# 128 instead of 96 tokens by gathered rows in an expert layer, and a ranking moved ahead of the transposes

## The chip, the core and the metric

The kernel runs on one core of a Trainium2 chip, as one launch. The metric is the device time of the launch in microseconds. The core has a matrix engine (PE, with its weight loads listed apart as PEld), a vector engine (DVE), a scalar engine (ACT), a general engine (POOL) and a queue that only issues transfers (SP). Each engine runs its instructions in program order. Sixteen DMA engines move the data; POOL's transfers stand in queue q0 (software), those of SP in q1 and those of ACT in q10 (hardware).

## What is computed

The reference is two transformer blocks on 512 tokens of width 1024. The change lies in the feed-forward layer of the first block, a layer of 16,384 experts. Each expert `e` has a row `u[e]` and a row `v[e]` of 1024 numbers:

```python
q = (xb @ wq).reshape(C, 8, 2, 64)
s = einsum('chpd,hpnd->chpn', q, keys)            # two lists of 128 scores per head
sv, si = top_k(s, 16)
cand = sv[:, :, 0, :, None] + sv[:, :, 1, None, :]
top_s, sel = top_k(cand.reshape(C, 8, 256), 16)   # 16 experts per head: 128 per token
g = softmax(top_s)
act = gelu(einsum('chkd,cd->chk', u_tab[eidx], xb))
out = einsum('chk,chkd->cd', g * act, v_tab[eidx])
```

## The kernel before

Products are made in two halves of each operand (high and low part), three matmuls for one. All weights come through one stream: SP loads a piece (`wr`), ACT casts its high part (`wh`, L119), DVE or POOL subtracts for the low part (`wl`, L121).

The expert layer treats tokens in two ways. **Dense tokens** (`TD`) are multiplied with all 16,384 experts, in 128 chunks of 128 experts, and the 128 wanted experts of a token are picked by a matrix `G` that is zero elsewhere. **Gathered tokens** (`GROUPS`, the last tokens) fetch only their own rows: an indirect DMA by POOL brings 128 rows of 4 KB (`row`, L935), and DVE does a dot product with it (`u` rows, L949) or adds it, weighted, to a sum (`v` rows, L958). A group of `n` tokens with `P` copies fills 128 partitions and needs 128/P such steps for `u` and as many for `v`: (64, 2) needs 64 + 64, and (32, 4) needs 32 + 32, so 192 steps before. The steps are a generator; `gstep()` does one of them at chosen places. One step keeps `GB - 1` = 2 loads ahead.

The layer has these stages, in program order:

- **The ahead stage.** For 84 of the chunks `u_chunk` multiplies the dense tokens with `u` (24 matmuls, L269, L270, L272), ACT applies gelu (L910), and the result is put away in DRAM (`ad`). Between chunks the generator `routing()` is pumped: it yields an estimate of DVE time after each part, and each chunk buys `BUD` of it; a `gstep` (at chunks whose number modulo 6 is in `GR`) costs 1.9. What is left when the chunks end is run off in a loop without chunks (`while live`). Routing goes through four tiles of 128 tokens, 3, 0, 1, 2. For each it ranks (`top16`, two heads at a time), decodes the winners to expert numbers (`id01`, with ACT's help at L1041 and L1045), lets PE transpose them (L1078), and builds for each 16 dense tokens four one-hot arrays on DVE (L1095 to L1101), from which PE makes a piece of `G` (`build_g`, 32 matmuls, L1113 and L1114); ACT evacuates it (L1115) and writes it to DRAM (`gd`). Tile 3 comes first because the gathered tokens lie in it: `pick` (L921) hands their expert numbers to the gathers.
- **The run stage.** Of the 44 fresh chunks, five `u_chunk`s open it. Then 16 runs of 8 chunks each follow, with the other 39 fresh chunks between their passes. A run has two passes over `v` (`v_pass`, 96 matmuls each at L260 to L262, one for each half of the width): a run in the middle of the stage is a pass, two fresh chunks, a pass, one fresh chunk. `load_g` loads the run's part of `G` (`gt`, on POOL's queue) a run ahead, `w_prod` (L1175) and `w_split` (L252, L253) make the weights of the experts, and DVE adds the products to the tokens (`hT`, L1206). A `gstep` follows each fresh chunk and those chunks of a pass that are in `GV`.
- Before the last pass, `while gat: gstep()` runs off the gather steps that are left, and the last of them ends in 8 or 16 matmuls on PE (L963) that fold the copies together.

Of the kernel before, what the change touches and what calls it, by code (L numbers as in the profile page):

```python
# [9 lines left out]
F32 = mybir.dt.float32  # L10
# [35 lines left out]
PRE = 2  # L46
BUD = 5.0
NA = 4
# [10 lines left out]
SUB = 16  # L59
GROUPS = ((64, 2), (32, 4))  # L60
TD = T - sum(n for n, _ in GROUPS)
NSB = TD // SUB
GR = (0, 3)
GB = 3
# [7 lines left out]
GP_ = 2  # L72
# [19 lines left out]
PA = tuple(range(6))  # L92
GV = (1, 2, 4, 6)

# [47 lines left out]
def _body(tc, nc, V, S, PE, GP, A, out, upto, tap, ctx):  # L142
# [106 lines left out]
    def split(hi, lo, src, g):  # L249

        if g is None:
            S.copy(hi, src)  # L252
            V.tensor_tensor(lo, src, r32(hi), op=OP.subtract)  # L253
        else:
            S.activation(hi, src, AF.Copy, scale=g)
            V.scalar_tensor_tensor(lo, src, g, r32(hi), op0=OP.mult, op1=OP.subtract)
# [88 lines left out]
    def xtile(p, h="xh", l="xl", n=8, c=T, bufs=None):  # L345
        return p.tile([128, n, c], F32R, name=h, bufs=bufs), p.tile([128, n, c], F32R, name=l, bufs=bufs)
# [429 lines left out]
    with ExitStack() as st:  # L776
        with st0 as st1:
            with ExitStack() as st2:
# [57 lines left out]
                if upto <= 1:  # L836
                    return dump()
                xnh, xnl = xtile(xp)
                gx = pool(st, "gx", side="right")
# [21 lines left out]
                def norm_x(k):  # L861
                    tn = xq.tile([128, T], F32, name="tn", bufs=2)
                    V.scalar_tensor_tensor(tn, H[k], col("g_ffn", k), rB[:, :T], op0=OP.mult, op1=OP.mult)
                    split(xnh[:, k], xnl[:, k], tn, None)
                    for a, (t0, n, P) in enumerate(groups):
                        V.tensor_copy(xg[:, a, k].rearrange("p (b t) -> p b t", b=P),
                                      tn[:, None, t0:t0 + n].to_broadcast([128, P, n]))
# [122 lines left out]

            def route(i):

                sv = wk.tile([128, 8, 2, 16], F32, name="sv", bufs=1)
                si = wk.tile([128, 8, 2, 16], U32, name="si", bufs=1)
                ts = wk.tile([128, 8, 16], F32, name="ts", bufs=1)
                tp = wk.tile([128, 8, 16], U32, name="tp", bufs=1)
                for h in range(0, 8, 2):
                    ch = []
# [20 lines left out]
                    top16(ch)  # L1019
                    yield 3.0  # L1020

                tpf = tp.rearrange("p h k -> p (h k)")
# [42 lines left out]
                V.tensor_tensor(ge, ge, gs[:, 1, :, None].to_broadcast([128, 8, 16]), op=OP.mult)  # L1065
                yield BUD
                if i == 3:
# [51 lines left out]
            def routing():  # L1119
                late = []  # L1120
                for i in (3, 0, 1, 2):
                    tk = yield from route(i)
                    for s in range(min(8, NSB - 8 * i)):
                        a = yield from onehots(tk, s)
                        late.append((i, s) + a)
                        if len(late) > 1:
                            build_g(*late.pop(0))
                for a in late:
                    build_g(*a)
# [30 lines left out]
        def load_g(r):  # L1160
            if r < len(runs):
                gt[r] = pk.tile([128, NSB, RUN, SUB], F32, name="gt", bufs=2)
                for b in range(0, NSB, NSB // GP_):
                    sl = slice(b, b + NSB // GP_)
                    nc.gpsimd.dma_start(gt[r][:, sl].rearrange("p b i t -> p b (i t)"),
                                        gd[sl, :, RUN * r:RUN * (r + 1)].rearrange("b p i t -> p b (i t)"))
# [738 lines left out]
```

## Time and profile before

| | |
|---|---|
| median of 3 runs | 2871.4 us (2870.38 to 2872.52) |
| the profiled execution, its time | 2870.35 us |
| its span, first to last instruction | 2868.2 us |
| PE busy | 2758.8 us, 96% |
| DVE busy | 1905.4 us, 66% |
| ACT busy | 1193.5 us, 42% |
| POOL busy | 876.0 us, 31% |
| moved by DMA | 457.17 MB, mean 159 GB/s |

Time outside the span is 2.15 us in the profiled execution. A busy share is a mean over stages that have different limits, so each stage is read by itself.

### The profile page before, as it was taken

The page shows a single profiled execution, that of the slowest core. Times are in us where ns is not written, and L with a number is a line of the kernel's source. Part 1 is how long each engine was busy: PE and PEld are TensorE (multiplying, and loading weights), DVE is VectorE, ACT ScalarE, POOL GpSimd, SP SyncE. Part 2 cuts the span into 40 slices and gives each one's busy share as a digit, 9 for nine tenths or more (in the row PEclk, how much of TensorE's full clock was granted, in tenths as well). Part 3 has the DMA queues.
Part 4 walks back from the last instruction along what each step waited for, and adds up shares of the span by engine and source line. Part 5 has one row for each costly group of instructions (what it writes and reads, how often), then busy time and mean ns, then how long its engine had stood idle before and what let it go on. Part 6 is the DMA issues. An engine that isn't in the chain of part 4 may idle for free. (4 is left out here: it accounts for less than half of the span.)

```text
span 2868.2 us, 38216 instructions
## 1 busy us (share of the span) xinstructions
PE 2758.8 (96%) x14308; PEld 2429.1 (85%) x14308; DVE 1905.4 (66%) x3477; ACT 1193.5 (42%) x1962; POOL 876.0 (31%) x521
## 2 busy tenths in 40 slices
PE   8778998999999999999999999999999999999998
PEld 7646898999989999999999988888887866788887
DVE  5887599798957867777778765444436489544433
ACT  5564543646553333343333423332223378433322
POOL 3653155555534456564456000000003133000000
PEclk9889999999999999999999999999999999999999
DMA  3102255767678888888888333333234200233332
GB/s 126 52 8 66 70 175 179 262 193 259 211 278 305 285 295 281 306 283 280 294 296 301 99 101 96 96 97 100 91 101 141 81 23 1 74 99 100 96 94 83
DMA packets 156568, 457.17 MB, mean 159 GB/s; under 512 B 17056, under 2 KB 40864, under 8 KB 152800
## 3 DMA queue, kind: packets, MB, share of 16 engines
q1 hardware_dynamic: 103008, 273.33, 29.5%
q0 software_dynamic: 36704, 135.54, 14.2%
q10 hardware_dynamic: 16672, 45.88, 4.0%
q8 instruction: 112, 1.84, 0.3%
q14 instruction: 72, 0.59, 0.1%
HBM read 407.43 MB, written 47.25 MB: 159 GB/s over the span
## 5 line engine op out<-in xcount | busy, mean ns | idle before, releaser
L119 ACT CAST wh<-wr 128x1024 fp32r<-128x1024 f32 (+1 forms) x356 | 369.4, 1038 | 394.4 <-issue 206.3
L121 DVE TENSOR_TENSOR wl<-wr,wh 128x1024 fp32r<-128x1024 f32 (+1 forms) x231 | 287.5, 1245 | 368.1 <-ACT wh L119 363.4
L121 POOL TENSOR_TENSOR wl<-wr,wh 128x1024 fp32r<-128x1024 f32 x125 | 334.0, 2673 | 330.2 <-ACT wh L119 325.4
L262 PE MATMUL m<-xh,wl 128*128 128x512 f32 x1080 | 422.2, 391 | 3.4 <-POOL wl L121 2.7
L260 PE MATMUL m<-xh,wh 128*128 128x512 f32 x1080 | 424.4, 393 | 0.0
L261 PE MATMUL m<-xl,wh 128*128 128x512 f32 x1048 | 407.9, 389 | 0.0
L269 PE MATMUL m<-xh,wh 128*128 128x416 f32 x1024 | 365.0, 356 | 9.7 <-ACT stg L1115 5.8
L261 PE MATMUL d<-wtl,vh 128*128 128x416 f32 x1024 | 359.5, 351 | 2.6 <-DVE wtl L253 2.6
L260 PE MATMUL d<-wth,vh 128*128 128x416 f32 x1024 | 359.8, 351 | 1.8 <-DVE hT L1206 0.9
L270 PE MATMUL m<-xl,wh 128*128 128x416 f32 x1024 | 360.9, 352 | 0.0
L262 PE MATMUL d<-wth,vl 128*128 128x416 f32 x1024 | 359.1, 351 | 0.2
L121 DVE TENSOR_TENSOR vl<-vr,vh 128x512 fp32r<-128x512 f32 x256 | 174.7, 688 | 140.1 <-ACT vh L119 133.9
L262 PEld LDWEIGHTS m<-xh,wl 128*128 128x128 f32 x1080 | 203.2, 188 | 49.4 <-DVE wl L121 3.4
L260 PEld LDWEIGHTS m<-xh,wh 128*128 128x128 f32 x1080 | 203.2, 188 | 43.3 <-issue 1.2
L119 ACT CAST vh<-vr 128x512 fp32r<-128x512 f32 x256 | 153.9, 619 | 206.1 <-DMA vr<-in_vr 148.5
L261 PEld LDWEIGHTS m<-xl,wh 128*128 128x128 f32 x1048 | 196.8, 188 | 41.2 <-issue 1.0
L935 POOL DMA_INDIRECT row<-in_vr,gix x96 | 174.6, 1818 | 141.0 <-DVE xt L958 109.3
L272 PE MATMUL m<-xh,wl 128*128 128x416 f32 x1024 | 213.3, 350 | 0.0
L910 ACT ACTIVATE act<-m 128x416 f32<-128x416 f32 x128 | 66.4, 519 | 343.3 <-PE m L272 336.5
L269 PEld LDWEIGHTS m<-xh,wh 128*128 128x128 f32 x1024 | 194.9, 190 | 15.8 <-ACT stg L1115 10.2
L261 PEld LDWEIGHTS d<-wtl,vh 128*128 128x128 f32 x1024 | 192.3, 188 | 5.5 <-DVE wtl L253 3.8
L260 PEld LDWEIGHTS d<-wth,vh 128*128 128x128 f32 x1024 | 192.2, 188 | 5.1 <-ACT act L910 1.3
(428 smaller groups left out, 5378.5 us busy)
## 6 DMA issues: line engine op xcount, KB each, us to landing
wr<-in_u SPq DMA_DIRECT2D x128, 512.0 KB
vr<-in_vr SPq DMA_DIRECT2D x256, 256.0 KB
wr<-in_w_gu SPq DMA_DIRECT2D x88, 512.0 KB
gd<-stg ACTq DMA_DIRECT2D x26, 1024.0 KB
gt<-gd POOLq DMA_DIRECT2D x32, 832.0 KB
ad<-act ACTq DMA_DIRECT2D x84, 208.0 KB
act<-ad SPq DMA_DIRECT2D x84, 208.0 KB
wr<-in_w_down SPq DMA_DIRECT2D x32, 512.0 KB
```

The lines of the kernel that those rows point to most:

```text
L119: nc.scalar.copy(hi[:, :n], t[:, :n])
L121: eng.tensor_tensor(lo[:, :n], t[:, :n], hi[:, :n].bitcast(F32), op=OP.subtract)
L260: PE.matmul(ps, lhsT=wh, rhs=xh, start=first, stop=False)
L261: PE.matmul(ps, lhsT=wh, rhs=xl, start=False, stop=False)
L262: PE.matmul(ps, lhsT=wl, rhs=xh, start=False, stop=last)
L269: PE.matmul(ps, lhsT=wh, rhs=xhs[k], start=k == 0, stop=False)
L270: PE.matmul(ps, lhsT=wh, rhs=xls[k], start=False, stop=False)
L272: PE.matmul(ps, lhsT=w[1][:, wc + k * 128:wc + k * 128 + 128], rhs=xhs[k], start=False, stop=k == n - 1)
L910: S.activation(a, ps, AF.Gelu)
L935: GP.indirect_dma_start(out=g, out_offset=None, in_=A["vr" if v else "ur"], in_offset=bass.IndirectOffsetOnAxis(ap=gix[:, a, j:j + 1], axi ...
```

## The change

One group of 32 gathered tokens becomes one of 64, so that all of tile 3 is gathered, the dense tokens go from 416 to 384, and the gather steps from 192 to 256. The places of gather steps are set closer (`GR`, `GV`), the budget of a chunk is made smaller (`BUD`), and `route` is cut into three generators (`rank`, `decode`, `turn`), so that the first two heads of the next tile are ranked between a tile's decoding and its transposes. The wait that a whole `BUD` stood for at the end of decoding becomes 1.0.

```diff
-BUD = 5.0
+BUD = 4.7
...
-GROUPS = ((64, 2), (32, 4))
+GROUPS = ((64, 2), (64, 2))
...
-GR = (0, 3)
+GR = (0, 2, 3, 5)
...
-GV = (1, 2, 4, 6)
+GV = (1, 2, 4, 5, 7)
...
-                xnh, xnl = xtile(xp)
+                xnh, xnl = xtile(xp, c=TD)
...
-                    split(xnh[:, k], xnl[:, k], tn, None)
+                    split(xnh[:, k], xnl[:, k], tn[:, :TD], None)
...
-                yield BUD
+                yield 1.0
+                return id01
+
+            def turn(i, id01):
+
                 if i == 3:
...
             def routing():
                 late = []
-                for i in (3, 0, 1, 2):
-                    tk = yield from route(i)
+                tiles = (3, 0, 1, 2)
+                yield from rank(3, range(0, 8, 2))
+                for n, i in enumerate(tiles):
+                    id01 = yield from decode(i)
+                    nxt = tiles[n + 1] if n < 3 else None
+                    if nxt is not None:
+                        yield from rank(nxt, (0,))
+                    tk = yield from turn(i, id01)
                     for s in range(min(8, NSB - 8 * i)):
                         a = yield from onehots(tk, s)
                         late.append((i, s) + a)
                         if len(late) > 1:
                             build_g(*late.pop(0))
+                    if nxt is not None:
+                        yield from rank(nxt, range(2, 8, 2))
                 for a in late:
                     build_g(*a)
```

`load_g` rounds its two parts up, which changes nothing at 24 pieces of 16 tokens (26 before).

**DVE, between the decoding of tile 0 and its one-hots.** Rows of before, then of the change: `id` holds the decoded expert numbers, `tk` their transposed copy, and L981 to L989 rank.

```order
L1064 RECIPROCAL gs<-gs 128x8
L1065 TENSOR_TENSOR id_4085<-id_4085,gs 128x128
L1082 SCALAR_TENSOR_TENSOR tk<-m,tk 128x128
L1095 TENSOR_TENSOR o_4257<-iop,tk 128x2048
L1097 TENSOR_TENSOR o_4258<-iop,tk 128x2048
L1099 TENSOR_TENSOR oh<-o_4258,tk 128x2048
L1101 TENSOR_TENSOR ol<-o_4258,tk 128x2048
```

```order
L1073 TENSOR_TENSOR id_4049<-id_4049,gs 128x128
L949 SCALAR_TENSOR_TENSOR row,gdt<-row,xt 128x1024
L981 MAX sv<-z_2392 128x8 x2
L983 MATCH_REPLACE tmp<-sv,z_2392 128x128 x2
L985 MAX_INDEX si<-sv,z_2392 128x8 x2
L987 MAX sv<-tmp 128x8 x2
L989 MAX_INDEX si<-sv,tmp 128x8 x2
L949 SCALAR_TENSOR_TENSOR row,gdt<-row,xt 128x1024
```

The ranking of tile 1's first two heads and two gather steps now stand between the last row of `id` and the row that reads the transposes (`tk`, L1094 now), 22 rows later instead of one.

**PE, at the last tile's transposes.** Before, these rows stand behind the 74th of the 84 chunks of the ahead stage, and a chunk follows. In the change they stand behind the 84th, and the pieces of `G` follow each other from there on (nine of them, L1125 and L1126 now) up to the first fresh chunk.

```order
L272 MATMUL m<-xh,wl 128x416 x8
L1078 MATMUL m<-ident,id_6962 128x128 x3
L269 MATMUL m<-xh,wh 128x416
L270 MATMUL m<-xl,wh 128x416
L269 MATMUL m<-xh,wh 128x416
```

```order
L272 MATMUL m<-xh,wl 128x384 x8
L1090 MATMUL m<-ident,id_7293 128x128 x3
L1125 LDWEIGHTS o_6781
L1125 MATMUL m<-oh,o_6781 128x128
L1126 LDWEIGHTS o_6781
L1126 MATMUL m<-ol,o_6781 128x128
```

So all eight one-hot sets of the last tile are made with no chunk left to run beside them; before, it was three of the four arrays of the last set.

**DVE, between the last two passes.** Before and in the change, from the last `v` split of the pass ahead to the first rows of the last pass; `xt` is the sum that a gather step of `v` adds to.

```order
L121 TENSOR_TENSOR vl<-vr,vh 128x512
L1206 TENSOR_TENSOR hT<-d,hT 128x2x416 x2
L966 TENSOR_TENSOR hT<-m,hT 128x8x32
L121 TENSOR_TENSOR wl<-wr,wh 128x1024
L121 TENSOR_TENSOR vl<-vr,vh 128x512 x2
```

```order
L958 SCALAR_TENSOR_TENSOR xt<-row,gdt,xt 128x1024
L1227 TENSOR_TENSOR hT<-d,hT 128x2x384 x2
L958 SCALAR_TENSOR_TENSOR xt<-row,gdt,xt 128x1024 x12
L966 TENSOR_TENSOR hT<-m,hT 128x8x64
L121 TENSOR_TENSOR wl<-wr,wh 128x1024
L121 TENSOR_TENSOR vl<-vr,vh 128x512 x2
```

Twelve gather steps, none before, are now run off in a row there; on PE the fold matmuls that wait for the last of them stand ahead of the last pass, before as in the change.

## Rows read from the trace of the kernel before

**Rows 1.** The page: span, and busy time of each engine.

```profile
span 2868.2 us, 38216 instructions
PE 2758.8 (96%) x14308; PEld 2429.1 (85%) x14308; DVE 1905.4 (66%) x3477; ACT 1193.5 (42%) x1962; POOL 876.0 (31%) x521
```

**Rows 2.** Busy time in five stretches, with PE's granted clock, DMA share, GB/s.

```profile
core 0: us, PE busy (x) PEld busy (x) DVE busy (x) ACT busy (x) POOL busy (x), PEclk, DMA share, GB/s
355.00:815.00 460.00, 436.43 (x2758) 422.21 (x2757) 397.80 (x1076) 233.15 (x288) 251.39 (x110) 0.98 0.65 215
815.00:830.00 15.00, 11.09 (x107) 10.23 (x105) 7.42 (x7) 11.80 (x14) 0.00 (x0) 0.77 0.89 332
848.00:1598.00 750.00, 745.42 (x3959) 736.30 (x3959) 568.23 (x807) 272.49 (x463) 396.12 (x232) 1.00 0.84 288
1000.00:1020.00 20.00, 20.00 (x108) 19.85 (x107) 13.67 (x21) 5.47 (x10) 6.36 (x6) 1.00 1.01 348
1400.00:1500.00 100.00, 100.00 (x533) 99.25 (x532) 75.11 (x111) 34.67 (x61) 49.34 (x30) 1.00 0.89 299
```

**Rows 3.** What PE waited for from 360 to 860: total us, times, longest.

```profile
PE m L1078 <- DVE id L1060: 9.6, 3, 4.9
```

**Rows 4.** Timeline of ACT in the ahead stage: start, length, instruction, idle before.

```profile
356.68 0.52 ACT L910 ACTIVATE act<-m 128x416 f32<-128x416 f32 x1 [1.26 <-PE m L272]
361.20 0.52 ACT L910 ACTIVATE act<-m 128x416 f32<-128x416 f32 x1 [2.48 <-PE m L272]
...
616.28 0.52 ACT L910 ACTIVATE act<-m 128x416 f32<-128x416 f32 x1 [2.50 <-PE m L272]
...
628.81 0.52 ACT L910 ACTIVATE act<-m 128x416 f32<-128x416 f32 x1 [5.61 <-PE m L272]
...
635.66 0.52 ACT L910 ACTIVATE act<-m 128x416 f32<-128x416 f32 x1 [0.62 <-PE m L272]
...
814.89 0.52 ACT L910 ACTIVATE act<-m 128x416 f32<-128x416 f32 x1 [0.63 <-PE m L272]
...
829.70 1.05 ACT L119 CAST wh<-wr 128x1024 fp32r<-128x1024 f32 x1 [0.40 <-ACT stg L1115]
```

**Rows 5.** Timeline of PE: three rows of equal matmuls, each row's first and last.

```profile
60.96 0.28 PE L398 MATMUL d<-xh,wh 128*128 128x264 f32 x1
...
64.48 0.28 PE L400 MATMUL d<-xh,wl 128*128 128x264 f32 x1
...
1099.76 0.35 PE L262 MATMUL d<-wth,vl 128*128 128x416 f32 x1
...
1103.93 0.35 PE L260 MATMUL d<-wth,vh 128*128 128x416 f32 x1
...
1899.83 0.39 PE L261 MATMUL m<-xl,wh 128*128 128x512 f32 x1
...
1903.90 0.39 PE L261 MATMUL m<-xl,wh 128*128 128x512 f32 x1
```

**Rows 6.** Groups of instructions, 600 to 1720: weight loads of the passes.

```profile
L262 PEld LDWEIGHTS d<-wth,vl 128*128 128x128 f32 x1024 | 192.2, 188 | 2.7 <-DVE vl L121 0.9
```

**Rows 7.** Timeline of DVE: first and last array of the last one-hot set.

```profile
817.71 1.22 DVE L1095 TENSOR_TENSOR o<-iop,tk 128x2048 f16<-128x2048 f16 x1
...
821.24 1.22 DVE L1101 TENSOR_TENSOR ol<-o,tk 128x2048 f16<-128x2048 f16 x1
```

**Rows 8.** DMA queues in one run, 997.8 to 1047.5: packets, MB, share of 16 engines.

```profile
DMA packets 5437, 14.14 MB, mean 284 GB/s; under 512 B 592, under 2 KB 1232, under 8 KB 5433
...
q0 software_dynamic: 1977, 7.25, 44.3%
q1 hardware_dynamic: 3456, 6.83, 38.8%
```

**Rows 9.** A gather: POOL's issue, and DVE's step that waited for it; DVE's group, 600 to 1720.

```profile
1049.70 1.17 POOL L935 DMA_INDIRECT row<-in_vr,gix  x1 [0.30 <-issue]
...
1061.13 1.28 DVE L958 SCALAR_TENSOR_TENSOR xt<-row,gdt,xt 128x1024 f32<-128x1024 f32 x1 [0.77 <-DMA row<-in_vr,gix]
...
L958 DVE SCALAR_TENSOR_TENSOR xt<-row,gdt,xt 128x1024 f32<-128x1024 f32 x94 | 127.4, 1355 | 6.3 <-DMA row<-in_vr,gix 6.2
```

More of the change, by code (lines that the diff above doesn't have):

```diff
@@ L989, in top16, with rank @@
                     V.max_index(di[:, 8:16], dv[:, 8:16], tmp)
[L991 to L997, printed above, removed]
+            rk = {}
+            def rank(i, heads):
+                if 0 in heads:
+                    rk[i] = (wk.tile([128, 8, 2, 16], F32, name="sv", bufs=1),
+                             wk.tile([128, 8, 2, 16], U32, name="si", bufs=1),
+                             wk.tile([128, 8, 16], F32, name="ts", bufs=1),
+                             wk.tile([128, 8, 16], U32, name="tp", bufs=1))
+                sv, si, ts, tp = rk[i]
+                for h in heads:
                     ch = []
@@ L1020, in route, with decode @@
                     yield 3.0
+            def decode(i):
+                sv, si, ts, tp = rk.pop(i)
                 tpf = tp.rearrange("p h k -> p (h k)")
@@ L1162, in load_g @@
                 gt[r] = pk.tile([128, NSB, RUN, SUB], F32, name="gt", bufs=2)
-                for b in range(0, NSB, NSB // GP_):
-                    sl = slice(b, b + NSB // GP_)
+                m = -(-NSB // GP_)
+                for b in range(0, NSB, m):
+                    sl = slice(b, min(b + m, NSB))
                     nc.gpsimd.dma_start(gt[r][:, sl].rearrange("p b i t -> p b (i t)"),
```

## The prediction

> **What bounds the kernel now.** The page first: PE is busy 96% of the span and DVE 66% [rows 1], so the question for each stage is whether PE has work all the time. The busy time by stretch shows two regimes [rows 2]. In the run stage, 848 to 1598, PE is busy 745 of 750 us at full clock: it is the bound there. In the ahead stage, 355 to 815, it is busy 436 of 460 us at a mean granted clock of 0.98, so some 24 us are gaps; the last stretch of it, 815 to 830, has PE busy 11 of 15 us at a clock of 0.77. The waits name the largest of these gaps: PE waited 9.6 us in three places for DVE's `id` before the transposes, up to 4.9 us each [rows 3]. ACT's timeline shows what such a place costs in all. A chunk takes 4.52 us from one gelu to the next (356.68 to 361.20), but 12.53 us where transposes stand between (616.28 to 628.81), and 6.85 us where a piece of `G` does (628.81 to 635.66) [rows 4]. The piece thus costs 2.33 us. From one chunk before the first gelu, 352.16, to the last at 814.89 are 462.7 us: 84 x 4.52 = 379.7, 23 pieces x 2.33 = 53.6, and a rest of 29.4 us, the waits around transposes and rankings.
>
> The DMA engines are the second bound, and a close one. In the run stage their share is 0.84, with 20 us stretches at 1.01 and 348 GB/s; the busiest 100 us, 1400 to 1500, have 0.89, and PE did not stop in them [rows 2].
>
> **Narrower matmuls.** What a matmul costs is the distance of starts, not its length, since they overlap. From the first and last rows: 264 columns, 29 steps in 3.52 us, 121.4 ns; 416 columns, 22 steps in 4.17 us, 189.5 ns; 512 columns, 18 steps in 4.07 us, 226.1 ns [rows 5]. A column costs 0.448 ns between 264 and 416, and 0.381 ns between 416 and 512. For 32 columns that is 14.3 or 12.2 ns. 384 lies between 264 and 416, so I take 14.2 ns. The straight line from 264 to 512, which leaves 416 above it, would give 17.4 ns; 12.2 and 17.4 are the ends. There are 6 x 1024 such matmuls, 87 us in all (75 to 107) if PE stays the bound: 84 x 24 of them in the ahead stage, 28.6 us, and 44 x 24 + 32 x 96 = 4128 in the run stage, 58.6 us.
>
> The Trainium skill, "TensorE: Matmul & The Clock Gate", section "Back-to-back issue gap", gives 81 ns a matmul at 128 columns and 131 ns at 512 for a stream of loads and matmuls; by that a column costs 0.13 ns, and the sum would have 26 us in the place of 87. The rows of this kernel contradict it, 226.1 ns at 512.
>
> **The ahead stage.** Besides the 28.6 us:
> - Two pieces of `G` fewer (24 for 26): 2 x 2.33 = 4.7 us saved.
> - The ranking between decoding and transposes. PE no longer reaches the transposes before `id`, since some two chunks lie between. But DVE is not faster: it gets 45 gather steps in this stage where it had 24, at 1.2 us or more each, some 25 us more in the same chunks, now 4.18 us long. What is late next is the one-hots, and behind them the first piece of `G` of a tile. I take 8 us off the rest of 29.4, which is about the 9.6 us of the named waits; the ends are 25 us gained (all waits gone) and 8 us lost (each tile's lag met in full at its `G`). POOL's low parts for the next chunk queue behind gather loads that wait for DVE; that lies inside these ends.
> - The tail. All eight one-hot sets of tile 2 stand behind the last chunk. An array follows the last at 1.18 us (817.71 to 821.24 in three steps [rows 7]), a set in 4.7 us. Eight take 38 us, then a last piece with its evacuation some 4 us: 42 us. Nine pieces of PE work, 21 us, lie in it, so 21 us are bare. Before, the tail from 814.89 to 829.70 was 14.8 us [rows 4] with three pieces, 7.0 us, in it: 7.8 us bare. The change loses 13 us; with POOL blocking DVE, or evacuation as the pace, up to 25.
>
> Sum for the ahead stage: -28.6 - 4.7 - 8 + 13 = **-28 us**.
>
> **The run stage.** One run, 997.8 to 1047.5, has 264 matmuls in 49.7 us. At 14.2 ns less each, PE needs 45.9 us. In it q0 moved 7.25 MB in 44.3% of 49.7 us, 22.0 us (329 GB/s), q1 6.83 MB in 38.8%, 19.3 us [rows 8]. The change puts 13 gather steps in a run for 11 (5 + 5 + 3 for 4 + 4 + 3), 0.524 MB each, takes 0.13 MB from `gt` and 0.08 MB from `ad`: q0 24.8 us, q1 19.1 us, with 0.3 of instructions 44.2 us. The DMA would have to be busy 96% of PE's time. One pass at 1.01 shows that it can be for 20 us [rows 2]; nothing shows it for 750. Loads that wait for their buffers leave holes in each run, and `gt`, 1.57 MB, stands ahead of gathers in the same queue: the gather issued at 1049.70 behind it was used at 1061.13, and DVE had waited 0.77 us for it [rows 9]. With steps nearer to each other such waits grow; DVE has some idle time to give in the first pass of a run, and `v` is split two chunks ahead of PE. I take 1 us of lost time a run, 16 us, so the run stage gains 58.6 - 16 = **43 us**. The ends: no loss, 59 us (with 17.4 ns a matmul 72 us), and 0.89, the share of the busiest 100 us, as the limit: 44.2 / 0.89 = 49.7 us, no gain at all.
>
> **Twelve steps before the last pass.** 45 steps in the ahead stage, 44 after fresh chunks and 5 x 31 in passes leave 12 of the 256 for the place where all are run off. DVE can do one in 1.2 to 1.36 us [rows 9], but each needs a load, and only three buffers go round. The lower end is 12 x 1.2 = 14 us; the upper is the loaded case, 11.4 us from issue to use with three in a round, 3.6 us each, 43 us. The queues are nearly empty by then: `gt` and `u` are loaded. 0.524 MB at the 348 GB/s of [rows 2] is 1.5 us, which is nearer to the lower end; I take 1.8 us, 22 us. PE has no cover: the fold matmuls, which wait for the last step, stand ahead of the pass. Behind such a gap PE starts at a lower clock (0.77 in the gap of 815 to 830 [rows 2]); I add 2 us. **+24 us**, from 15 to 45.
>
> The Trainium skill, "DMA: Bandwidth & Descriptors", section "Anatomy of one DMA — SWDGE (gpsimd) path", has 2.0 us + bytes / 436e3 for a transfer from this queue, an estimate of 3.2 us for a gather; with issue and step that makes 1.9 us each in a round of three, and the sum 1 us longer. No run here shows it.
>
> Nothing else has a price: the narrower splits of `xnh` and `xnl`, evacuations, products and adds lie on ACT and DVE beside PE's matmuls. Without that cover they would save a few us, not cost any.
>
> **Sum.** 2870.35 - 28 - 43 + 24 = 2823 us on the profiled execution's own time, which is 1 us under the median of the runs shown: **2824 us**.
>
> **The rivals.**
> - *PE keeps all of it.* The DMA fills its holes, the run stage gains 59 us, the ahead stage 40, and the run-off costs 16: 2787 us. For it speaks PE unbroken at a share of 0.89; against it the sums at 96%.
> - *The DMA becomes the bound, slower than before.* With everything else as forecast, a run must take 50.0 us to eat the gain; that is a share of 0.88. If a mixed load holds only the 0.84 that it holds now on the mean, a run takes 52.6 us, 2.9 more than before: 2870 - 28 + 47 + 24 = 2913 us; at 0.86 it is 2893. For it speaks that no stretch of 100 us is over 0.89; against it, that in those stretches PE set the pace and not the DMA.
> - *The weight load sets the pace of a matmul.* Each has one, of 188 ns on the mean [rows 6], as long as the 189 ns between starts. Then fewer columns buy nothing: 2870 - 4.7 - 8 + 13 + 24 = 2894 us. Against it: the 264 columns at 121 ns [rows 5] have the same loads. The skill's page named above says that both set the spacing.
> - *The change does not give the saving it buys*: as forecast, with a run at 49.7 us: 2866 us.
>
> **How the numbers follow.** The forecast 0.6, all kept 0.2, no gain in the run stage 0.1, DMA-bound and slower 0.08, the weight load 0.02. The range has to leave out 2 in 10: 2795 at the low end cuts off the better half of the first rival, and 2868 at the high end takes in the fourth and leaves out the slower ones. Within 0.2%, about what a measurement of this kernel can tell from no change, is 2865.7 to 2877.1; half of the fourth rival falls in it, 0.05. Faster 0.85, slower 0.1.
>
> **What would show it.** Starts of 384-column matmuls 173 to 176 ns apart. Runs of 46 to 48 us with a DMA share over 0.9, and a few us of waits for `vl` or `wth`. Nine pieces of `G` in a row in some 42 us. A gap on PE of some 24 us before the last pass, behind L966's sum. The forecast is wrong if runs stay near 50 us with a share under 0.9, if one-hots stall chunks by more than 10 us a tile, or if the run-off takes over 40 us.

## The result, and the profile after

The changed kernel takes **2913.6 us**, the kernel before 2872.0 us beside it: 1.0143 times as long, 95% interval 1.013 to 1.0156. The forecast was 2824 us, faster. The time of the rival "the DMA becomes the bound", 2913 us, was hit to the microsecond, but the experiments show that its mechanism is not what happened; the hit was luck.

The page of the profiled execution, 2914.3 us in all, its span and busy times, answers to [rows 1]: PE has 48 us less to do in a span that is 44 us longer.

```profile
span 2912.4 us, 38321 instructions
PE 2710.3 (93%) x14241; PEld 2368.8 (81%) x14241; DVE 2012.3 (69%) x3560; ACT 1175.6 (40%) x1952; POOL 959.8 (33%) x585
```

Busy times by stretch (beside [rows 2]): the ahead stage up to the last chunk, its tail of one-hots, the early chunks, the run stage, and the gap before the last pass.

```profile
core 0: us, PE busy (x) PEld busy (x) DVE busy (x) ACT busy (x) POOL busy (x), PEclk, DMA share, GB/s
355.00:781.00 426.00, 396.41 (x2504) 381.31 (x2503) 413.27 (x1088) 202.84 (x254) 292.13 (x131) 0.98 0.73 239
781.00:822.00 41.00, 26.52 (x288) 23.71 (x287) 37.34 (x33) 32.33 (x37) 0.00 (x0) 0.75 0.49 198
822.00:845.00 23.00, 21.96 (x125) 21.64 (x122) 11.65 (x17) 9.29 (x15) 6.10 (x5) 0.96 0.90 320
845.00:1610.00 765.00, 710.53 (x3928) 694.94 (x3928) 611.97 (x840) 262.45 (x459) 431.18 (x264) 0.97 0.86 298
1610.00:1638.30 28.30, 0.36 (x3) 0.04 (x2) 17.79 (x15) 0.91 (x2) 9.39 (x10) 0.60 0.71 239
```

PE no longer fills the run stage: 710.5 of 765 us, where before it had 745.4 of 750. The passes start at 845 us (850.7 before) and the last one but one ends at 1610 (1596 before): the ahead stage gained 6 us, the run stage lost 20, and then come 28 us without work on PE, at a clock of 0.60. What PE waited for from 340 to 1750 says where (total us, times, longest):

```profile
PE d L262 <- DVE vl L121: 40.6, 16, 4.1
PE m L963 <- DVE xt L958: 27.9, 1, 27.9
PE d L260 <- ACT vh L119: 9.1, 7, 4.5
PE m L272 <- POOL wl L121: 7.8, 5, 4.8
```

Nothing of this size stood in the run stage before. The matmuls themselves are as forecast; two starts of PE's timeline in an undisturbed pass, eleven steps apart, give 1.90 / 11 = 173 ns ([rows 5] had 189.5):

```profile
1284.82 0.33 PE L262 MATMUL d<-wth,vl 128*128 128x384 f32 x1
...
1286.72 0.33 PE L261 MATMUL d<-wtl,vh 128*128 128x384 f32 x1
```

A second pass takes the 16.8 us that this gives. Runs 2 to 15 have a first pass of 19.5 to 24.8 us; that of the 16th and last run, which has no `gt` left to load, takes 17.15 us. Here is a slow one, from 1250.70 to 1272.12: timeline rows of POOL, then ACT, then DVE, and PE's row (start, length, instruction, idle before).

```profile
1252.44 2.15 POOL L1186 DMA_DIRECT2D gt<-gd  x2
1254.90 1.60 POOL L935 DMA_INDIRECT row<-in_ur,gix  x1 [0.30 <-issue]
...
1261.80 0.62 ACT L119 CAST vh<-vr 128x512 fp32r<-128x512 f32 x1 [6.27 <-DMA vr<-in_vr]
...
1262.46 0.69 DVE L121 TENSOR_TENSOR vl<-vr,vh 128x512 fp32r<-128x512 f32 x1 [4.47 <-ACT vh L119]
1267.68 1.23 DVE L949 SCALAR_TENSOR_TENSOR row<-row,xt 128x1024 f32<-128x1024 f32 x1 [4.53 <-DMA row<-in_ur,gix]
1268.83 0.08 DVE L949 DVE_READ_ACCUMULATOR row<-row,xt 128x1 f32 x1
1268.83 0.69 DVE L121 TENSOR_TENSOR vl<-vr,vh 128x512 fp32r<-128x512 f32 x1
...
1269.58 0.44 PE L262 MATMUL d<-wth,vl 128*128 128x384 f32 x1 [3.78 <-DVE vl L121]
```

Read it upwards. PE waits 3.78 us for a `vl`. That `vl`, at 1268.83, waits for nothing of its own: it stands on DVE behind a gather step, and the step had waited 4.53 us for its row. The row had been asked for (1254.90) behind the 1.57 MB of `gt` in the same queue. `v` is split two chunks ahead, 2 x 12 x 174 ns = 4.2 us, but little of this lead was left when the row was late: a piece of `v` itself (`vr`) had come 6.27 us late, so the `vl` at 1262.46 was ready at 1263.15, 0.4 us before PE used it (1263.55). In all 14 slow passes DVE waited 2.4 to 5.2 us for one row. A late `vr` alone does little harm. In the kernel before, ACT waited for these pieces as long as now (before, then the change, from 850.7 to 1596 and from 845 to 1610), and PE waited for no `vl`; but there no row in a pass was late by more than 1.5 us.

```profile
ACT vh L119 <- DMA vr<-in_vr: 148.5, 72, 7.7
```

```profile
ACT vh L119 <- DMA vr<-in_vr: 151.5, 61, 8.6
```

The stop has a second price. Behind it PE works at a granted clock of 0.50, the lower of its two levels (1.2 GHz), where it had 1.00 ahead of it, and matmuls start 0.32 us apart instead of 0.17:

```profile
1252.00:1264.00 12.00, 12.00 (x71) 12.00 (x70) 6.09 (x11) 3.32 (x6) 6.56 (x6) 1.00 0.86 273
1271.00:1274.00 3.00, 3.00 (x11) 3.00 (x10) 3.00 (x3) 0.00 (x0) 2.75 (x2) 0.50 0.98 328
```

```profile
1271.28 0.52 PE L261 MATMUL d<-wtl,vh 128*128 128x384 f32 x1
1271.60 0.52 PE L262 MATMUL d<-wth,vl 128*128 128x384 f32 x1
```

This follows the stop in ten of the 14 passes. From 845 to 1610 PE waits 53 us in all, and 41 us are at 0.50, none before. By the distances of starts these 41 us cost some 19 us (an estimate).

### The profile page after: what moved, and what is told of

Its sections match the earlier page's. It is cut to its first block, busy times and chain, and to the rows that moved or that the text cites. A ratio compares the mean times of both kernels' runs of the same rounds, so it can differ in the third digit from the quotient of the medians.

```text
span 2912.4 us, 38321 instructions
## 1 busy us (share of the span) xinstructions
PE 2710.3 (93%) x14241; PEld 2368.8 (81%) x14241; DVE 2012.3 (69%) x3560; ACT 1175.6 (40%) x1952; POOL 959.8 (33%) x585
## 3 DMA queue, kind: packets, MB, share of 16 engines
q0 software_dynamic: 45408, 167.00, 16.9%
## 5 line engine op out<-in xcount | busy, mean ns | idle before, releaser
L262 PE MATMUL d<-wth,vl 128*128 128x384 f32 x1024 | 352.7, 344 | 41.5 <-DVE vl L121 40.6
L260 PE MATMUL d<-wth,vh 128*128 128x384 f32 x1024 | 350.0, 342 | 11.7 <-ACT vh L119 9.1
L269 PE MATMUL m<-xh,wh 128*128 128x384 f32 x1024 | 351.0, 343 | 7.9 <-ACT wh L119 4.8
L261 PE MATMUL d<-wtl,vh 128*128 128x384 f32 x1024 | 349.1, 341 | 2.3 <-DVE wtl L253 2.2
L270 PE MATMUL m<-xl,wh 128*128 128x384 f32 x1024 | 346.4, 338 | 0.0
L262 PEld LDWEIGHTS d<-wth,vl 128*128 128x128 f32 x1024 | 196.9, 192 | 51.3 <-DVE vl L121 51.0
L260 PEld LDWEIGHTS m<-xh,wh 128*128 128x128 f32 x1080 | 203.4, 188 | 43.1 <-issue 1.2
L949 DVE SCALAR_TENSOR_TENSOR row<-row,xt 128x1024 f32<-128x1024 f32 x128 | 211.8, 1658 | 30.3 <-DMA row<-in_ur,gix 30.2
L958 DVE SCALAR_TENSOR_TENSOR xt<-row,gdt,xt 128x1024 f32<-128x1024 f32 x126 | 192.7, 1529 | 45.2 <-DMA row<-in_vr,gix 43.8
L272 PE MATMUL m<-xh,wl 128*128 128x384 f32 x1024 | 202.1, 338 | 8.4 <-POOL wl L121 7.8
```

Source lines behind the costliest of these rows:

```text
L260: PE.matmul(ps, lhsT=wh, rhs=xh, start=first, stop=False)
L261: PE.matmul(ps, lhsT=wh, rhs=xl, start=False, stop=False)
L262: PE.matmul(ps, lhsT=wl, rhs=xh, start=False, stop=last)
L269: PE.matmul(ps, lhsT=wh, rhs=xhs[k], start=k == 0, stop=False)
L270: PE.matmul(ps, lhsT=wh, rhs=xls[k], start=False, stop=False)
L272: PE.matmul(ps, lhsT=w[1][:, wc + k * 128:wc + k * 128 + 128], rhs=xhs[k], start=False, stop=k == n - 1)
```

## The experiments

Every ratio is against the kernel before, run on the same chip. A line of a diff is against the changed kernel unless said otherwise. The theories: **A**, `gt` bunches the transfers of a run into a burst; **B**, DVE waits in its order for rows, and `vl` behind them is late; **C**, the rival of the forecast, the bytes of a run are too many; **D** and **F**, about the ahead stage, come below.

### The two halves of the change apart

The order alone, with 96 tokens and all constants of before:

```diff
-BUD = 4.7
+BUD = 5.0
-GROUPS = ((64, 2), (64, 2))
+GROUPS = ((64, 2), (32, 4))
-GR = (0, 2, 3, 5)
+GR = (0, 3)
-GV = (1, 2, 4, 5, 7)
+GV = (1, 2, 4, 6)
```

> One part alone: 96 tokens gathered and 416 dense with the constants of before, and only the order of the routing changed (the next tile's first two heads ranked between a tile's decoding and its transposes, the other six behind its one-hots). Theory (the order is worth little, since the same DVE work has to be done before the same last G piece, and what it moves is waited for elsewhere): 2872 +- 4 us, last G piece near 827 us as in before. Rival (the term of the prediction, -8 us, is right and the loss lies wholly in the 128 tokens): 2864 +- 3 us, and the waits of the transposes (L1078 of before) gone without a new one.

2873.0 us against 2870.6, ratio 1.0011 (1.0001 to 1.0021). The order gains nothing. It is not idle: the last piece of `G` ends at 813 us instead of 826, but chunks that had stood ahead of it now follow it, and the passes start at 847.9 instead of 850.7. Those 3 us go at the other end, where the last gather step comes 2.3 us late for the fold. The waits for `id` fell only from 9.6 us [rows 3] to 7.5, and the one for `eg`, the expert numbers that `pick` takes, rose from 2.4 to 5.3.

The 128 tokens alone, in the old order:

```diff
-                yield from rank(3, range(0, 8, 2))
                 for n, i in enumerate(tiles):
+                    yield from rank(i, range(0, 8, 2))
                     id01 = yield from decode(i)
-                    nxt = tiles[n + 1] if n < 3 else None
+                    nxt = None
```

> The other part alone: 128 tokens gathered and 384 dense with the constants of the change, and the routing in the order of before (a tile ranked whole, decoded, transposed). Theory (the 128 tokens make the loss, the order is worth little): 2913 to 2922 us. Rival (the order itself costs, since it puts ranking ahead of the one-hots that TensorE waits for): 2895 to 2908 us, with the last G piece earlier than 822 us.

2908.0 us, ratio 1.0129 (1.0108 to 1.0149), last piece of `G` at 822.3 as in the changed kernel. The time is 5 us under the theory's range and at the upper end of the rival's, but the rival's earlier `G` did not come, and the interval overlaps that of the changed kernel. The loss belongs to the 128 tokens and the constants that go with them.

### What slows a first pass

The `gt` load half a run earlier:

```diff
             if r:
-                load_g(r + 1)
+                pass
...
+            steps.setdefault(0, []).append((load_g, r + 2))
             v_pass(r, 1, steps, enter if last else None)
```

> One wait moved: the load of gt for a run (1.57 MB on the software queue of the gathers) is asked for half a run earlier, at the start of the second pass of the run before and no longer at the start of the first pass ahead of the gathers. Nothing is left out. Theory A (a burst: gt, gathers, V pieces and u weights meet at the start of a first pass and delay each other, while the transfers of a whole run would fit): first passes fall from 19.5..24.8 us to about 17..18.5, second passes stay near 16.7..17.5, a run falls from 50.7 to about 47.5, time 2860 to 2880 us. Theory C (the bytes of a run alone are too many): a run stays near 50 us, the waits for vl move to the second passes, time 2905 to 2920 us. Theory B (a gather has too few buffers and VectorE waits for each row in its order): waits of xt and row for DMA stay as they are (69 us together), time 2895 to 2915 us.

2906.3 us, ratio 1.0125 (1.0109 to 1.0142). The slow pass moved with `gt`: second passes now take 18.4 to 23.5 us, and most first passes 16.83. So `gt` decides which pass is slow, but a pass with all of `gt` in it is slow wherever it is. Theory A is right about what makes the pass slow, and its forecast for this remedy fell; the time lies in the ranges of B and C, which this run does not tell apart.

The gather steps of the run stage left out:

```diff
             aw[c] = u_chunk(c, pk, 6)
-            gstep(GU)
...
-                if j in GV:
-                    gstep()
...
-                while gat:
-                    gstep()
```

> A probe: the gather steps of the run stage are left out (those beside the ahead chunks stay), so the last 128 tokens get a wrong sum; all else as in the changed kernel. It shows what a run costs without 12 gathers of 0.5 MB and their VectorE work. Theory (TensorE alone needs 45.9 us a run): runs of 46 to 46.7 us, second and first passes alike 16.7 us, no wait for vl, run stage 765 -> 700..710 us (the first run is longer), no run-off: 2913 - 60 - 30 = about 2823 us, range 2805 to 2840. Rival (gt, V and u already collide without gathers): first passes stay at 18 us or more, 2850 us or more.

2795.4 us, ratio 0.9739 (0.9719 to 0.9758), and in the run stage no wait for `vl` or `vh`. A run takes 45.86 us (passes from 1206.64 to 1252.50): the 45.9 us of PE's work that the forecast gave it. The time is 28 us under my sum, because the gathers had cost the run stage 80 us (685.7 now for 765.4) and not the 60 I took for them.

Rows loaded, but not used by DVE:

```diff
                     L = 128 // P
-                    if not v:
+                    if pr and not (v and j == 0):
+                        pass
+                    elif not v:
...
+        pr.append(1)
```

> A probe: in the run stage the gathered rows are still loaded, one a step, but VectorE no longer multiplies or adds them (the last 128 tokens get a wrong sum); a buffer comes free when its last load has landed. It takes VectorE's wait for rows and its 1.2 us a step away and keeps every byte. Theory B (the wait of VectorE in its order is what holds vl up): passes as without gathers, 16.83 us, and 2800 to 2815 us. Theories A and C (the DMA engines are full, V pieces land late): first passes still 19 us or more, with PE waiting for vl or vh whose wait is now for the transfer of vr; 2860 us or more.

2808.1 us, ratio 0.9777 (0.9757 to 0.9796). All transfers are there, and the stretch of the run stage has PE at work 657 of 660 us while the DMA carries 332 GB/s:

```profile
860.00:1520.00 660.00, 657.25 (x3761) 652.62 (x3760) 324.53 (x535) 246.94 (x430) 321.02 (x253) 1.00 0.93 332
```

The same stretch of the changed kernel had less of both:

```profile
860.00:1520.00 660.00, 611.59 (x3388) 599.27 (x3388) 520.49 (x722) 224.17 (x390) 377.44 (x231) 0.97 0.86 299
```

So the DMA engines are not the limit at a share of 0.86; theory C falls. This run took DVE's work away with its wait, though, so it does not tell the two apart. The next two keep the work.

`gt` in four parts of 0.39 MB, two in each pass:

```diff
+GA = ((0, 2), (4, 3))
+GB2 = ((0, 0), (4, 1))
...
-                load_g(r + 1)
+                steps0 = {j: [(lambda q, n=r + 1: load_g(n, (q,)), q)] for j, q in GA}
...
+            for j, q in GB2:
+                steps.setdefault(j, []).append((lambda q, n=r + 2: load_g(n, (q,)), q))
             v_pass(r, 1, steps, enter if last else None)
```

> The gt load of a run is cut in four parts of 0.39 MB and asked for one part at a time, two in the second pass of the run before and two in the first pass, each behind a gather. Nothing is left out. Moving the whole load (the run before this one) only moved the slow pass: 22 us where gt lands, 16.83 us in the other. Theory A (a pass can carry its V pieces, its five gathers and half of gt: 2.1 + 2.6 + 0.8 MB in 16.8 us is 327 GB/s, and 322 to 404 GB/s were seen): all passes 16.8 to 18 us, time 2850 to 2880 us. Theory C (the bytes of a run are too many wherever they lie): both passes near 19 us, time 2900 to 2915 us.

2853.3 us, ratio 0.9940 (0.9924 to 0.9957): 60 us less than the changed kernel from the same bytes in other places, and faster than before. Nearly all passes take 16.83 to 17.1 us.

One buffer more for rows:

```diff
-                    g = gx.tile([128, 1024], F32, name="row", bufs=GB)
+                    rb["c"] += 1
+                    if rb["p"] is not None and rb["c"] % 4 == 3:
+                        g = rb["p"].tile([128, 1024], F32, name="row", bufs=1)
+                    else:
+                        g = gx.tile([128, 1024], F32, name="row", bufs=GB)
...
-                    if n + GB - 1 < len(todo):
-                        load(*todo[n + GB - 1])
+                    while nl < min(n + rb["n"], len(todo)):
+                        load(*todo[nl])
+                        nl += 1
...
+        rb.update(p=pk, n=4)
```

> One buffer more for gathered rows in the run stage (four where there were three, so a row is asked for three steps ahead). Nothing is left out. Theory B (VectorE stands at a late row in its order, and vl behind it comes late): the waits of xt and row for DMA fall from 69 us to under 35 us, first passes to 17..19 us, time 2865 to 2890 us. Theories A and C (the transfers themselves are late, so one row more in flight only makes the V pieces later): within 8 us of the changed kernel, 2905 to 2920 us, with more of the wait on vh for the V pieces.

2856.8 us, ratio 0.9954 (0.9937 to 0.9970): as good, with `gt` still asked for all at once and pieces of `v` still up to 7.7 us late. Two edits with nothing in common but that rows come in time for DVE both take the loss away. The two theories are halves of one: `gt` makes the rows behind it late (A), and DVE's order makes `vl` late with them (B). DVE's waits for rows from 845 to 1610 show what counts. The changed kernel, then the one with `gt` in parts:

```profile
DVE xt L958 <- DMA row<-in_vr,gix: 33.5, 11, 5.2
DVE row L949 <- DMA row<-in_ur,gix: 25.1, 9, 4.5
```

```profile
DVE xt L960 <- DMA row<-in_vr,gix: 31.5, 34, 1.8
DVE row L951 <- DMA row<-in_ur,gix: 11.2, 17, 1.1
```

The sum (69 us with those at the end of the stage, as the expectations count it) only falls from 58.6 to 42.7 us, of which 10 lie behind the passes, in the steps run off. But the longest wait falls from 5.2 to 1.8, and PE's wait for `vl` from 40.6 to 2.9 us. With five steps a pass, waits of up to some 2 us within a pass hide in the lead by which `v` is split ahead; in the changed kernel none of 2.4 us or more did.

A control with 96 tokens (the first kernel above) and `gt` in parts:

> A control: 96 tokens gathered and 416 dense with the constants of before (routing in the new order, which alone measured 2873 us), and gt in four parts over two passes. Nothing is left out. Theory (there TensorE is busy throughout the run stage, so late rows cost it nothing): 2866 to 2873 us. Rival (gt in parts helps any version by the same 60 us): 2810 to 2830 us.

2875.3 us, ratio 1.0016 (1.0007 to 1.0026), 2 us above the theory's range. Where PE was never stopped, the edit gains nothing.

### The twelve steps at the end

In the changed kernel the steps run off start 2.2 us apart, eleven distances between these two rows of DVE. With a fourth row buffer (the kernel with one buffer more, above) it is 1.8 us.

```profile
1612.39 1.27 DVE L958 SCALAR_TENSOR_TENSOR xt<-row,gdt,xt 128x1024 f32<-128x1024 f32 x1
...
1636.93 1.28 DVE L958 SCALAR_TENSOR_TENSOR xt<-row,gdt,xt 128x1024 f32<-128x1024 f32 x1 [1.61 <-DMA row<-in_vr,gix]
```

A sixth step in each second pass takes them away:

```diff
+GV2 = (0, 1, 2, 4, 5, 7)
...
-                if j in GV:
+                if j in (GV, GV2)[h]:
```

> One gather step more in every second pass (six instead of five, first passes keep five), so that no step is left before the last pass. Nothing is left out. Theory (the steps left over cost their 28 us of idle TensorE and the slow clock behind it, and second passes have room): the idle stretch before the last pass goes, 2880 to 2890 us. Rival (each step added to a second pass costs as much there, about 2 us): second passes 17.5 to 19 us, 2905 us or more.

2913.5 us, ratio 1.0142 (1.0125 to 1.0159). The gap is gone, and nothing is won: PE's wait for `vl` rises from 40.6 to 55.7 us. The rival held while rows are late. With rows in time (four parts, four buffers, and the sixth step):

> The three edits of the run stage together: gt in four parts over two passes, four row buffers, and a sixth gather step in each second pass so that none is left before the last pass. Nothing is left out. Theory B (rows late in VectorE's order held vl up; with rows in time a pass has room for a sixth step): passes 16.8 to 17.3 us, no idle stretch before the last pass, 2820 to 2832 us. Rival (a sixth step still costs its 2 us, as it did with gt in one piece): 2848 to 2860 us.

2820.5 us, ratio 0.9815 (0.9797 to 0.9832): 33 us below the kernel with `gt` in parts alone. In the stretch of the run stage DVE works more than in the changed kernel, and PE hardly stops:

```profile
860.00:1520.00 660.00, 651.35 (x3715) 644.40 (x3714) 551.93 (x800) 244.21 (x427) 450.74 (x296) 1.00 0.95 339
```

The DMA holds a share of 0.95 over 660 us. This comes close to the 96% that the forecast doubted ("nothing shows it for 750").

### The ahead stage

**Theory D**: DVE bounds it. In the windows above DVE is busy 413 + 37 of 467 us there. No gather steps in the stage:

```diff
-GR = (0, 2, 3, 5)
+GR = ()
```

> The changed kernel with no gather step in the ahead stage (56 fewer there), all of them left to the idle stretch before the last pass. Nothing is left out; what is read is the time of the last G piece. Theory D (VectorE bounds the ahead stage; a gather step takes 1.23 us of it, 69 us in all, until TensorE's 423 us bind): the last G piece lands at 775 to 790 us instead of 822. Rival (TensorE's matmuls bound it, as the prediction had it, and the eight one-hot sets behind the last chunk stay): 810 to 822 us. The whole takes about 2 us more for each of the 56 steps at the end, so 2980 to 3000 us with theory D.

The last piece of `G` ends at 760.5 us, 62 us earlier, but that overstates the gain: eleven of the 84 chunks, which all stood ahead of that piece, now follow it. The passes start at 830.0 us instead of 844.9, and these 15 us are what the steps had cost (45 of them by the trace, not 56). Theory D holds so far and no further: from 355 to 830 DVE is now busy 361 of 475 us and PE 440, so neither fills the stage, and the 32 to 47 us that I gave did not come. The run also took the loads of rows off POOL's queue, so it does not tell DVE's time from those. The whole, 3003 us in one run, pays with 130 us of gap at the end.

Does it pay to move chunks, or steps? Both on the kernel with the three edits:

```diff
-EXTRA = 4
+EXTRA = 8
```

> As the kernel with the three edits of the run stage, and 12 more hidden chunks computed in the ahead stage (96 instead of 84, so 32 fresh ones in the runs instead of 44). Nothing is left out. Theory D (VectorE bounds the ahead stage: 450.6 us busy of 467, TensorE 422.9, so TensorE's idle 44 us there can carry some ten chunks of 4.18 us): the last G piece lands at 828 to 842 us, the run stage is 50 us shorter, 2785 to 2800 us. Rival (TensorE's idle time there can't be filled, since the one-hots of the tail still come after the last chunk): the last G piece at 862 us or more, within 8 us of the kernel with 84 chunks ahead.

2823.7 us, ratio 0.9828 (0.9810 to 0.9846), not told apart from 2820.5. The expectation had the edit wrong: it moves 4 chunks (88 ahead, 40 fresh), not 12. They moved the last piece of `G` from 822.6 to 836.2, and the start of the passes as much, most of the 16.7 us that they cost PE (4 x 4.18). The idle time there did not carry them, which speaks against DVE as the only bound of the stage.

```diff
-GR = (0, 2, 3, 5)
+GR = (0, 2, 4)
-GV = (1, 2, 4, 5, 7)
+GV = (0, 1, 2, 4, 5, 7)
```

> The kernel with the three edits of the run stage, with a gather step beside 3 of 6 ahead chunks instead of 4 of 6 (14 fewer of 56) and six in every pass. Nothing is left out. Theory D (a step costs VectorE 1.1 us in the ahead stage, which it bounds, and nothing in a pass whose rows come in time): last G piece at 807 to 812 us, passes 16.8 to 17.2 us, 2803 to 2812 us. Rival E (a sixth step in a first pass makes rows late again): first passes 18 us or more, 2818 to 2835 us.

2826.4 us, ratio 0.9847 (0.9830 to 0.9863); last piece of `G` at 813.8, passes from 837.0. And with `GR = (0, 3)` and seven steps in a second pass:

> The same with a gather step beside 2 of 6 ahead chunks, as in before (28 fewer of 56), six in a first pass and seven in a second. Nothing is left out. Theory D: last G piece at 790 to 797 us, about 28 us earlier than in the changed kernel, which is the whole of the forecast gain that was missing; passes 16.8 to 17.3 us, 2788 to 2800 us. Rival E (a run of 46 us has no room for 15 gathers of 0.5 MB, 16.5 MB in all, 359 GB/s): passes 18 us or more and waits of TensorE for vl, 2815 us or more.

2833.2 us, ratio 0.9868 (0.9851 to 0.9884); last piece at 804.0, passes from 828.7 (845.7 with the three edits alone). The stage has 34 and 23 steps by the trace where it had 45; it gets 9 and 17 us, less than expected, and the run stage gives them back with interest: second passes with seven steps mostly take 17.6 to 19.9 us, PE waiting 18.2 us in 28 places for `vl`. Rows are hardly late there (11 us of waits in all, none over 1.3), yet PE's longer stops, of 0.9 to 1.7 us, stand just behind such waits: with DVE busy 16.9 of 19.1 us in such a pass even a short wait is not hidden. The DMA share is 0.95. Which of these sets 19 us was not tried.

**Theory F**: what a gather step costs there. DVE's groups from 340 to 822 (total us, mean ns) give it 2.03 us, not 1.2:

```profile
L949 DVE SCALAR_TENSOR_TENSOR row<-row,xt 128x1024 f32<-128x1024 f32 x45 | 91.3, 2029 | 0.0
```

The kernel before had 24 of them at 1.79 us:

```profile
L949 DVE SCALAR_TENSOR_TENSOR row<-row,xt 128x1024 f32<-128x1024 f32 x24 | 42.9, 1789 | 0.0
```

The timelines of DVE and then of POOL, in the changed kernel, show two steps, each of which starts beside a subtraction of POOL and ends 1.08 us after that is over:

```profile
701.57 3.41 DVE L949 SCALAR_TENSOR_TENSOR row<-row,xt 128x1024 f32<-128x1024 f32 x1
...
706.05 3.40 DVE L949 SCALAR_TENSOR_TENSOR row<-row,xt 128x1024 f32<-128x1024 f32 x1
```

```profile
700.96 2.94 POOL L121 TENSOR_TENSOR wl<-wr,wh 128x1024 fp32r<-128x1024 f32 x1 [3.93 <-ACT wh L119]
...
705.83 2.54 POOL L121 TENSOR_TENSOR wl<-wr,wh 128x1024 fp32r<-128x1024 f32 x1
```

Take POOL's part away, and give it to DVE:

```diff
-PA = tuple(range(6))
+PA = ()
```

> The changed kernel with the low parts of all ahead u chunks made on VectorE, none on GpSimd. Nothing is left out. What is read is the length of a gather step (row<-row,xt on VectorE) in the ahead stage. Theory F (VectorE and GpSimd hold each other up when both read two tensors): all steps there 1.2 to 1.3 us, the mean falls from 2.03 us, 36 us of VectorE time come back, while 84 subtractions of 1.2 us, 100 us, are added to VectorE: the stage ends about 60 us later, 2960 to 2985 us in all. Rival (a step is slow because of its row or its accumulator): the mean stays at 1.8 us or more.

```profile
L121 DVE TENSOR_TENSOR wl<-wr,wh 128x1024 fp32r<-128x1024 f32 x87 | 105.7, 1215 | 35.0 <-ACT wh L119 34.8
L949 DVE SCALAR_TENSOR_TENSOR row<-row,xt 128x1024 f32<-128x1024 f32 x47 | 57.2, 1217 | 0.0
```

A step takes 1.22 us on the mean. And the stage did not grow by 60 us: its last piece of `G` came 8 us earlier, at 814.1, and the passes started 8 us earlier, at 836.9, with 87 subtractions on DVE in this window where there had been one. From 355 to 822 DVE is busy 427 us where it was 451, since its one-hots, too, are no longer held up. The whole took 2899.5 us in its single run. On the kernel with the three edits:

> The kernel with the three edits of the run stage (2820 us), and the low parts of the ahead u chunks made on VectorE, none on GpSimd. Nothing is left out. Theory F (GpSimd's subtractions hold VectorE up by more than their own 1.22 us on VectorE): last G piece at 814 us instead of 822, 2806 to 2815 us. Rival (the single look before was a fast draw, and TensorE's waits for wl of 13 us eat it): 2816 to 2826 us.

2814.1 us, ratio 0.9801 (0.9784 to 0.9817), last piece of `G` at 813.9, passes from 836.4. That and the next are the fastest here, though their intervals overlap that of 2820.5 us. With the fresh chunks' low parts on DVE as well (`PF = 99`):

> As the run before it, with the low parts of the fresh chunks and of all later u chunks on VectorE as well. Nothing is left out. Theory F in the run stage too (a subtraction of 2.7 us on GpSimd holds up gather steps and vl there): VectorE's share falls or stays, runs stay at 45.9 to 46.5 us, within 5 us of the run before it, since TensorE is already the bound there. Rival (39 more operations on VectorE make vl late again): runs of 47 us or more, 8 us or more slower than the run before it.

2813.8 us, ratio 0.9798 (0.9782 to 0.9815): no difference shows, and PE is busy 653 and 654 of the 660 us from 860 in the two.

## Why the prediction was wrong

**The step that failed** is in the run stage: "DVE has some idle time to give in the first pass of a run, and `v` is split two chunks ahead of PE. I take 1 us of lost time a run". Without any loss the stage, from the first pass to the end of the last first pass, would have taken 745.4 - 58.6 = 686.8 us (685.7 with the gathers left out); it took 765.4. The loss was 79 us for 16, almost five a run. Rows in time bring 61 of them back (704.7 us, 845.7 to 1550.4), 4.3 us for each of the 14 slow runs, and what then remains, 18 us, is about what I took. PE's stops and the lower clock behind them, 53 us and some 19, make up most of the 79. The sentence adds up idle time; what counts is the length of one wait against the cover that is left when it comes, 4.2 us at the most. The example that I quoted in the same place, a gather issued behind `gt` and used 11 us later [rows 9], was the mechanism itself. Before, it cost nothing, for its wait was 0.77 us; now the waits were 2.4 to 5.2 us. That five steps in a pass for four are what made them so long is argued: no run has 128 tokens and four. One of the forecast's own signs of being wrong came: a run of 51.6 us (passes from 1199.07 to 1250.70) at a share of 0.86.

**The other terms:**
- *Narrower matmuls*: right, 173 ns, and a run of 45.9 us without gathers. With rows in time the run stage gained 745.4 - 704.7 = 41 us, for 43 forecast with ends of 0 and 59.
- *The ahead stage*: 6 us gained for 28. The tail was right (41 us for 42, nine pieces, counted from the first of them at 781). The part ahead of it was not: "I take 8 us off the rest of 29.4". By the same count the rest is now 781 - 352 - 84 x 4.18 - 15 x 2.2 = 45 us: 15 more, not 8 less. The term behind it is "45 gather steps where it had 24, at 1.2 us or more each, some 25 us more". DVE's groups have 91.3 us in these steps now and 42.9 before, 48 more, since POOL held them up. What the added steps cost is measured: with 23 of them instead of 45 the passes start 17 us earlier, and that is most of the 22 us missing. With none they start no earlier than with 23 (830.0 and 828.7), so the other 5 us or so have another cause, which stays open. POOL's part in the length of a step is shown; with steps of 1.22 us the passes start 8 and 9 us earlier.
- *The steps run off at the end*: 28 us of gap, and a fold that took 3.7 us at the low clock for 1.9; 30 us with it, for 24 forecast with ends of 15 and 45. A step came every 2.2 us, where I had taken 1.8. The Trainium skill's figure for this queue, "DMA: Bandwidth & Descriptors", section "Anatomy of one DMA — SWDGE (gpsimd) path", had given an estimate of 1.9 us; the trace has 0.3 us more.
- *The rivals*: "the DMA becomes the bound" gave 2913 us by taking the mean share of 0.84 for what a mixed load holds. The share was indeed 0.86, but as a consequence: with rows in time the same engines held 0.95. A share measured while something else sets the pace is no limit. "The weight load sets the pace" is refuted by 173 ns.

**The sum as measured**: -5.8 in the ahead stage, +20.0 in the run stage, +30.5 for the run-off and the last pass's slow start make +44.7 at the end of the last pass (1660.7 for 1616.0), and 2914.3 - 2870.4 = 44 in all. The forecast had -28 - 43 + 24. Of the 91 us between, the run stage holds 63, the ahead stage 22, the run-off 6.

## What to carry to other kernels

Where one engine both waits for transfers in its program order and prepares another engine's operands, look at the single waits and not at their sum beside the idle time: compare a wait with the lead of the preparation that is left at that moment, which other late transfers may have eaten, and count what the engine loses at a lower clock behind a stop. Here a large transfer in the queue of small urgent ones made the single wait long; cutting it in parts or giving the urgent ones a buffer more cured it. When you measure how long a stage takes, end it where its successor starts: an inner event such as the last piece of `G` moves when work changes places. Before you believe that the DMA is the bound, find out whether its share is the cause or the consequence, by leaving out the use of the data and keeping the transfers. Work handed from DVE to an idle POOL is not free for DVE: look at what DVE's own operations last beside it.

## What the hardware showed that was not expected

- DVE's gather step with two inputs hardly moves on while a subtraction of POOL runs: 3.41 us with 2.33 us of it beside a subtraction, 1.22 us on the mean of 47 without any. The Trainium skill, "SBUF — State Buffer", section "🔬 SBUF: two separate sides", describes one port pair shared by the two engines as a lock held for a whole instruction, under which the other one blocks; the trace agrees for these operations. Here it made the hand-over a loss: with 84 subtractions less to do DVE was busy 24 us longer (451 us for 427).
- A mixed load of gathers of 4 KB rows, `gt`, `v` and `u` pieces held a DMA share of 0.95 at 339 GB/s over 660 us, above any 100 us of the kernel before (0.89).
